# A norm's sum over the partitions: two dense products with ones, and the root on all partitions

## The chip, the cores and the metric

The kernel runs on one core of a Trainium2 chip. The metric is the time of one execution on the device in microseconds; the time of a kernel is the median of its runs. Five engines work side by side, each in the order of its own queue: TensorE (PE; its weight loads are shown as PEld), VectorE (DVE), ScalarE (ACT), GpSimd (POOL) and SyncE (SP, which here issues DMAs).

## The reference

The reference is an encoder of two layers on 512 positions of 1024 features. Each layer is a SwiGLU half-step, a mixer with three branches (a gated DeltaNet, pooling, dilated attention) and a second SwiGLU half-step. What matters here is the norm ahead of each of the three parts:

```python
def _rmsnorm(x, gain):
    xf = x.astype(jnp.float32)
    y = xf * lax.rsqrt(jnp.mean(xf * xf, axis=-1, keepdims=True) + RMS_EPS)
    return (y * gain.astype(jnp.float32)).astype(x.dtype)

for l in range(DEPTH):                      # DEPTH = 2
    x = x + 0.5 * _swiglu(_rmsnorm(x, ffn1_norm[l]), ...)
    h = _rmsnorm(x, mix_norm[l])
    ...
    x = x + 0.5 * _swiglu(_rmsnorm(x, ffn2_norm[l]), ...)
return _rmsnorm(x, final_norm)
```

## The kernel before

The activations lie with features on the partitions and positions along the columns: eight tiles `xs` of 128 x 512. A gemm (L238 to L253) makes one 128 x 512 output tile. Its operands are split into a high and a low part of type fp32r (`split`, L186: ScalarE rounds to the high part at L187, VectorE subtracts at L188). For each of the k blocks it issues three products, high by high (L246), high by low (L248) and low by high (L250); with the eight blocks of `xs` these are 24 products. The accumulator is one of three PSUM banks (pool `psA`). The weights come by DMA in blocks of 1024 columns and are split into pairs of 512 columns, of which four can stand ready (`weights`, L190, with the tags `wh` and `wl`).

The norm is not applied to the operand. `prep` (L257) multiplies a tile by the gain, splits it, and adds its squares to `ss` (128 x 512) by `square` (L264). The gemms work on the unnormed tiles, and each output column is multiplied by the factor R of its position when the accumulator is read out: L308 and L312 in the FFN, L407 and L375 in the mixer, L1085 for the gates. R is a 128 x 512 tile with the same row on all partitions.

`norm` (L285) computes R from `ss`. It calls `rms` (L289). For each of four blocks of 128 positions, that function multiplies a block of `ss` by a column of ones (L294), which puts the sum of each position on a partition of its own, in one column. The four columns go through mean and epsilon (L296) and through `rsqrt_cols` (L272: root on ScalarE, reciprocal and one Newton step on VectorE), all 128 x 4. Four transposes (L300) of the columns, each spread over 128, bring the factors back along the columns on all partitions, and L287 copies them into R. The last norm of the kernel is done by `down_last` (L332), which calls `rms` itself.

A planner of the framework sets the order on each engine from the order of the program, with an offset for parts marked as urgent (`high_priority`); `norm` and the read-outs of the mixer carry the largest offset, `AHEAD_E`, and the weights a smaller one, `AHEAD`. Within one queue an instruction that waits holds up all behind it. Tiles with the tag `t` (`T5`, `tt`) share four buffers, small PSUM tiles (`bank`) five.

In the mixer, `deltanet` (L386) begins with a short gemm for beta and decay (L404, L405), read out with R at L407. Then comes a chain of small steps on PE, DVE and ACT (L410 to L458), and then the twelve convolutions (`conv`, L370), each on a gemm's output, read out with R at L375 into a tile `t`.

Of the kernel before, what the change touches and what calls it, by code (L numbers as in the profile page):

```python
# [10 lines left out]
F32 = mybir.dt.float32  # L11
F32R = mybir.dt.float32r
AF = mybir.ActivationFunctionType
ALU = mybir.AluOpType
AX = mybir.AxisListType

P = 128
T = 512
D = 1024
# [4 lines left out]
RMS_EPS = 1e-6  # L24
# [77 lines left out]
def trunk(ctx: ExitStack, tc: tile.TileContext, A, out):  # L102
    nc = tc.nc
    V, S, G, PE = nc.vector, nc.scalar, nc.gpsimd, nc.tensor
    PSUM = bass.MemoryType.PSUM

    pc = ctx.enter_context(tc.tile_pool(name="pc", bufs=1))
# [11 lines left out]
    def nm(s):  # L119
        uid[0] += 1  # L120
        return f"{s}_{uid[0]}"

    def T5(dt=F32):
        return pt_.tile([P, TW], dt, tag="t", name=nm("t"))

    def tt():
        return T5()[:, 0:T]
# [10 lines left out]
    def bank():  # L138
        return psM.tile([P, T], F32, tag="m", name=nm("m"))

    def small(w, tag, bufs=2):
        return pc.tile([P, w], F32, tag=tag, bufs=bufs, name=nm(tag))

    def f32(ap):
        return ap.bitcast(F32)
# [4 lines left out]

    cst = pc.tile([P, NCONST], F32, name="cst")
    gain = pc.tile([P, (3 * DEPTH + 1) * NB], F32, name="gain")
    pc.tile([P, 8], F32, name="pad")
    eps = pc.tile([P, 2], F32, name="eps")
    V.memset(eps[:, 0:1], RMS_EPS)
    V.memset(eps[:, 1:2], 4.0 * L2_EPS)
    ones = pc.tile([P, 2], F32, name="ones")
    V.memset(ones, 1.0)

    def C(n):  # L160
        o, w = CONST[n]
        return cst[:, o:o + w]
# [5 lines left out]
    ss = pc.tile([P, T], F32, name="ss")  # L168
    R = pc.tile([P, T], F32, name="R")
# [16 lines left out]
    def split(raw, h, l):  # L186
        S.activation(h, raw, AF.Copy)  # L187
        V.tensor_tensor(out=l, in0=raw, in1=f32(h), op=ALU.subtract)  # L188
# [83 lines left out]
    def rsqrt_cols(v, n):  # L272
        y = small(n, "rs1")
        u = small(n, "rs2")
        S.activation(u, v, AF.Sqrt)  # L275
        V.reciprocal(y, u)  # L276
        V.scalar_tensor_tensor(out=u, in0=y, scalar=-0.5, in1=y, op0=ALU.mult, op1=ALU.mult)
        V.tensor_tensor(out=u, in0=u, in1=v, op=ALU.mult)
        V.scalar_tensor_tensor(out=y, in0=u, scalar=1.5, in1=y, op0=ALU.add, op1=ALU.mult)
        return y  # L280
# [2 lines left out]
        S.activation(small(1, "jk"), col, AF.Sqrt, scale=0.0, bias=ones[:, 0:1])  # L283

    def norm():  # L285
        with tc.high_priority(offset=AHEAD_E):
            V.tensor_copy(R, rms([ss], 0, 4))  # L287

    def rms(parts, b0, b1):  # L289
        n = b1 - b0  # L290
        p = bank()
        for b in range(b0, b1):
            for i, t in enumerate(parts):
                PE.matmul(p[:, b:b + 1], t[:, b * P:(b + 1) * P], ones[:, 0:1], start=(i == 0), stop=(i == len(parts) - 1))  # L294
        v = small(4, "nv")[:, 0:n]
        V.tensor_scalar(out=v, in0=p[:, b0:b1], scalar1=1.0 / D, scalar2=RMS_EPS, op0=ALU.mult, op1=ALU.add)  # L296
        y = rsqrt_cols(v, n)
        q = bank()
        for b in range(n):
            PE.transpose(q[:, b * P:(b + 1) * P], y[:, b:b + 1].to_broadcast([P, P]), ident)  # L300
        return q[:, 0:n * P]
# [889 lines left out]
    for l in range(DEPTH):  # L1191
        norm()
        ffn(A["f1g"][l], A["f1u"][l], A["f1d"][l], xs, 3 * l + 1, True)
        norm()
        xs = mixer(l, 3 * l + 2)
        norm()
        last = l == DEPTH - 1
        ffn(A["f2g"][l], A["f2u"][l], A["f2d"][l], xs, None if last else 3 * l + 3, False)
# [59 lines left out]
```

## Time and profile before

| | |
|---|---|
| median of 3 runs | 2571.84 us (2570.33 to 2571.87) |
| profiled execution | 2572.03 us |
| its span | 2570.2 us |
| instructions | 33959 |
| PE, PEld | 2548.9 us (99%), 2087.2 us (81%) |
| DVE, ACT, POOL | 1469.6 us (57%), 1002.9 us (39%), 164.0 us (6%) |

The span is the time between the first and the last instruction that the profile shows. Busy time is the time in which an engine has at least one instruction under way. Matmuls overlap, so that their durations add up to more than the time they take; what a matmul costs is the distance from one start to the next. In a timeline, the first number is the start in us from the start of the span, the second the duration.

### The profile page before, as it was taken

The numbers are of one execution on the slowest core, as the hardware profiler recorded it, in microseconds if no ns is written. First come the engines' busy times: TensorE is split into PE (matmuls) and PEld (weight loads), VectorE is DVE, ScalarE is ACT, GpSimd is POOL, SyncE is SP. The second block draws the span as 40 slices with busy tenths as digits, with TensorE's granted clock in tenths as the row PEclk, the third lists the DMA queues.
The fourth block names the chain that finished last, engine by engine and source line by source line (L and its number), as shares of the span: only waits on it lengthen the run. The fifth ranks groups of instructions, "written<-read, shape, count | busy, mean of one in ns | idle before, by whom it ended". The sixth has DMA issues, their size and how long they took to land. (4 is left out here: it accounts for less than half of the span.)

```text
span 2570.2 us, 33959 instructions
## 1 busy us (share of the span) xinstructions
PE 2548.9 (99%) x13018; PEld 2087.2 (81%) x13018; DVE 1469.6 (57%) x2702; ACT 1002.9 (39%) x1946; POOL 164.0 (6%) x117
## 2 busy tenths in 40 slices
PE   9999999999999999999999999999999999999998
PEld 7888887888878788888888888878888778888887
DVE  6444349956767654443444444499566576544433
ACT  5333234464443333333233332354644334333322
POOL 1000000001221200000000000000022112000010
PEclk9999999999999999999999999999999999999999
DMA  4222333232323522223322223323323244222232
GB/s 157 97 99 97 113 104 107 89 119 88 109 90 111 171 95 99 98 92 96 101 97 93 98 97 117 110 97 100 107 94 103 83 136 155 91 99 98 96 96 80
DMA packets 96051, 268.32 MB, mean 104 GB/s; under 512 B 14384, under 2 KB 19984, under 8 KB 95888
## 3 DMA queue, kind: packets, MB, share of 16 engines
q1 hardware_dynamic: 74928, 229.41, 27.1%
q10 hardware_dynamic: 20960, 36.75, 4.5%
q8 instruction: 102, 1.67, 0.3%
q14 instruction: 61, 0.50, 0.1%
HBM read 245.02 MB, written 14.79 MB: 101 GB/s over the span
## 5 line engine op out<-in xcount | busy, mean ns | idle before, releaser
L187 ACT ACTIVATE wh<-raw 128x512 fp32r<-128x512 f32 (+1 forms) x870 | 539.1, 620 | 1171.7 <-PE acc L248 1097.0
L250 PE MATMUL acc<-xh,wl 128*128 128x512 f32 x2400 | 941.1, 392 | 1.5 <-DVE wl L188 1.5
L246 PE MATMUL acc<-xh,wh 128*128 128x512 f32 x2400 | 940.7, 392 | 1.4 <-ACT wh L187 1.1
L248 PE MATMUL acc<-xl,wh 128*128 128x512 f32 x2400 | 939.9, 392 | 0.5 <-DVE xl L1175 0.3
L188 DVE TENSOR_TENSOR wl<-raw,wh 128x512 fp32r<-128x512 f32 (+1 forms) x870 | 604.2, 694 | 540.2 <-ACT wh L187 534.9
L250 PEld LDWEIGHTS acc<-xh,wl 128*128 128x128 f32 x2400 | 451.0, 188 | 99.0 <-issue 3.5
L246 PEld LDWEIGHTS acc<-xh,wh 128*128 128x128 f32 x2400 | 451.1, 188 | 98.9 <-issue 2.9
L248 PEld LDWEIGHTS acc<-xl,wh 128*128 128x128 f32 x2400 | 450.8, 188 | 97.1 <-issue 2.6
L246 PE MATMUL acc<-r,wh 128*128 128x512 f32 x970 | 379.2, 391 | 6.9 <-DVE f L1137 6.9
L250 PE MATMUL acc<-r,wl 128*128 128x512 f32 x970 | 379.1, 391 | 0.0
L248 PE MATMUL acc<-r,wh 128*128 128x512 f32 x970 | 379.0, 391 | 0.0
L246 PEld LDWEIGHTS acc<-r,wh 128*128 128x128 f32 x970 | 182.9, 189 | 46.1 <-issue 7.7
L248 PEld LDWEIGHTS acc<-r,wh 128*128 128x128 f32 x970 | 182.7, 188 | 38.3 <-issue 0.3
L250 PEld LDWEIGHTS acc<-r,wl 128*128 128x128 f32 x970 | 182.9, 189 | 38.1
L312 DVE TENSOR_TENSOR t<-acc,R 128x512 f32<-128x512 f32 x88 | 60.9, 692 | 132.1 <-PE acc L250 132.1
L308 DVE TENSOR_TENSOR f<-acc,R 128x512 f32<-128x512 f32 x88 | 60.9, 692 | 128.1 <-PE acc L250 127.9
L187 ACT ACTIVATE r<-t 128x512 fp32r<-128x512 f32 x96 | 60.4, 631 | 128.6 <-DVE t L313 127.5
L188 DVE TENSOR_TENSOR r<-t,r 128x512 fp32r<-128x512 f32 x96 | 69.8, 729 | 60.8 <-ACT r L187 60.7
L591 POOL MEMSET r<- 128x1024 f32 x2 | 1.9, 953 | 1107.9 <-PE acc L250 1107.9
L379 DVE SCALAR_TENSOR_TENSOR f<-t,cw,f 128x512 f32<-128x512 f32 x96 | 69.4, 744 | 0.0
L309 ACT ACTIVATE f<-f 128x512 f32<-128x512 f32 x88 | 55.7, 632 | 23.0 <-DVE f L308 23.0
L313 DVE TENSOR_TENSOR t<-t,f 128x512 f32<-128x512 f32 x88 | 60.5, 688 | 1.3 <-ACT f L309 1.3
(281 smaller groups left out, 1692.8 us busy)
## 6 DMA issues: line engine op xcount, KB each, us to landing
raw<-in_win_dram SPq DMA_DIRECT2D x76, 512.0 KB, 3.3
raw<-in_wgt_dram SPq DMA_DIRECT2D x48, 512.0 KB, 3.3
raw<-in_f2g_dram SPq DMA_DIRECT2D x44, 512.0 KB, 3.2
raw<-in_f2u_dram SPq DMA_DIRECT2D x44, 512.0 KB, 3.2
raw<-in_f1g_dram SPq DMA_DIRECT2D x43, 512.0 KB, 3.2
raw<-in_f1u_dram SPq DMA_DIRECT2D x43, 512.0 KB, 3.2
raw<-in_f1d_dram SPq DMA_DIRECT2D x32, 512.0 KB, 3.4
raw<-in_f2d_dram SPq DMA_DIRECT2D x32, 512.0 KB, 3.5
```

The costliest lines, as they stand in the source:

```text
L187: S.activation(h, raw, AF.Copy)
L188: V.tensor_tensor(out=l, in0=raw, in1=f32(h), op=ALU.subtract)
L246: PE.matmul(acc, a, h, start=(k == 0), stop=False)
L248: PE.matmul(acc, a, l, start=False, stop=False)
L250: last = PE.matmul(acc, b, h, start=False, stop=(k == nk - 1))
L308: V.tensor_tensor(out=g1, in0=g, in1=R, op=ALU.mult)
L309: S.activation(g1, g1, AF.Silu)
L312: V.tensor_tensor(out=u1, in0=u, in1=R, op=ALU.mult)
L313: V.tensor_tensor(out=u1, in0=u1, in1=g1, op=ALU.mult)
L379: V.scalar_tensor_tensor(out=a, in0=cp[:, j:j + T], scalar=w[:, j:j + 1], in1=a, op0=ALU.mult, op1=ALU.add)
L591: G.memset(X_, 0.0)
```

## The change

Only `norm` is changed. The tile `pad`, which nothing used, gives way to `onesr`, ones of type fp32r. `ss` is split into a high and a low part (128 x 512 each); both are multiplied by a 128 x 128 matrix of ones, made by repeating one column of `onesr`, and accumulated in one PSUM bank. This puts the sum of each position on all partitions at once. Mean and epsilon, the root, the reciprocal and the Newton step then run on the full 128 x 512 tile and end in R. The transposes and the copy L287 are gone from `norm`; `rms` stays for the last tile.

```diff
-    pc.tile([P, 8], F32, name="pad")
+    onesr = pc.tile([P, 2], F32R, name="onesr")
...
     V.memset(ones, 1.0)
+    V.tensor_copy(onesr, ones)
...
     def norm():
+
         with tc.high_priority(offset=AHEAD_E):
-            V.tensor_copy(R, rms([ss], 0, 4))
+            h, lo = T5(F32R)[:, 0:T], T5(F32R)[:, 0:T]
+            split(ss, h, lo)
+            p = bank()
+            on = onesr[:, 0:1].to_broadcast([P, P])
+            PE.matmul(p, on, h, start=True, stop=False)
+            PE.matmul(p, on, lo, start=False, stop=True)
+            V.tensor_scalar(out=ss, in0=p, scalar1=1.0 / D, scalar2=RMS_EPS, op0=ALU.mult, op1=ALU.add)
+            u = tt()
+            S.activation(u, ss, AF.Sqrt)
+            V.reciprocal(R, u)
+            V.scalar_tensor_tensor(out=u, in0=R, scalar=-0.5, in1=R, op0=ALU.mult, op1=ALU.mult)
+            V.tensor_tensor(out=u, in0=u, in1=ss, op=ALU.mult)
+            V.scalar_tensor_tensor(out=R, in0=u, scalar=1.5, in1=R, op0=ALU.add, op1=ALU.mult)
```

## Rows read from the trace of the kernel before

**Rows 1.** Page, part 1 (busy) and part 2 (TensorE's granted clock).

```profile
PE 2548.9 (99%) x13018; PEld 2087.2 (81%) x13018; DVE 1469.6 (57%) x2702; ACT 1002.9 (39%) x1946; POOL 164.0 (6%) x117
...
PEclk9999999999999999999999999999999999999999
```

**Rows 2.** Waits of TensorE: line, releaser, total us, times, longest.

```profile
PE acc L246 <- ACT wh L187: 1.1, 2, 0.5
```

**Rows 3.** Groups by line and shape, TensorE, the two lines of the old norm.

```profile
L294 PE MATMUL m<-ones,ss 128*128 128x1 f32 x56 | 7.5, 247 | 0.0
...
L300 PE MATMUL m<-ident,rs 128*128 128x128 f32 x28 | 4.6, 282 | 1.4 <-DVE rs L279 1.4
```

**Rows 4.** Timeline of TensorE, norm ahead of the second FFN: start, duration.

```profile
923.42 0.39 PE L246 MATMUL acc<-xh,wh 128*128 128x512 f32 x1
...
926.05 1.02 PE L294 MATMUL m<-ones,ss 128*128 128x1 f32 x8
...
933.44 0.39 PE L248 MATMUL acc<-xl,wh 128*128 128x512 f32 x1
...
944.55 0.39 PE L250 MATMUL acc<-xh,wl 128*128 128x512 f32 x1
```

**Rows 5.** Groups by line and shape, VectorE: busy us, mean ns of one.

```profile
L260 DVE SCALAR_TENSOR_TENSOR xl<-mg,gain,xh 128x512 fp32r<-128x512 f32 x40 | 29.9, 748 | 0.2
L270 DVE TENSOR_TENSOR ss<-ss,t 128x512 f32<-128x512 f32 x41 | 28.2, 689 | 0.6
...
L287 DVE COPY R<-m 128x512 f32<-128x512 f32 x6 | 4.1, 687 | 0.9 <-PE m L300 0.9
...
L276 DVE RECIPROCAL rs<-rs 128x4 f32<-128x4 f32 x6 | 1.1, 176 | 0.8 <-ACT rs L275 0.5
L276 DVE RECIPROCAL rs<-rs 128x16 f32<-128x16 f32 x4 | 1.0, 250 | 2.7 <-ACT rs L275 2.7
...
L430 DVE RECIPROCAL sp<-sp 128x32 f32<-128x32 f32 x2 | 0.7, 353 | 2.3 <-ACT sp L427 2.3
```

**Rows 6.** Groups by line and shape, ScalarE.

```profile
L187 ACT ACTIVATE wh<-raw 128x512 fp32r<-128x512 f32 x823 | 519.6, 631 | 1081.5 <-PE acc L248 1011.0 <-DVE wl L188 23.3 <-issue 10.3
```

**Rows 7.** Timeline of VectorE, the same norm as rows 4.

```profile
925.22 0.69 DVE L270 TENSOR_TENSOR ss<-ss,t 128x512 f32<-128x512 f32 x1
...
932.05 0.69 DVE L308 TENSOR_TENSOR f<-acc,R 128x512 f32<-128x512 f32 x1
```

**Rows 8.** Timeline of VectorE, norm ahead of the mixer, and after it.

```profile
373.37 0.69 DVE L270 TENSOR_TENSOR ss<-ss,t 128x512 f32<-128x512 f32 x1
...
377.71 0.68 DVE L287 COPY R<-m 128x512 f32<-128x512 f32 x1
...
389.05 0.28 DVE L458 COPY t<-m 32x128 f32<-32x128 f32 x1 [0.39 <-PE m L456]
389.27 0.67 DVE L375 TENSOR_TENSOR t<-acc,R 128x512 f32<-128x512 f32 x1
...
427.31 0.69 DVE L375 TENSOR_TENSOR t<-acc,R 128x512 f32<-128x512 f32 x1
```

**Rows 9.** Window of VectorE between the last two rows: length, busy us.

```profile
389.27:427.31 38.04, 34.70 (x65) 1.00 0.35 112
```

**Rows 10.** Timeline of TensorE around the end of that window.

```profile
427.23 0.39 PE L250 MATMUL acc<-xh,wl 128*128 128x512 f32 x1
428.15 0.47 PE L246 MATMUL acc<-xh,wh 128*128 128x512 f32 x1 [0.53 <-ACT wh L187]
```

**Rows 11.** Timeline of VectorE, the kernel's first norm.

```profile
18.99 0.68 DVE L1185 TENSOR_TENSOR ss<-ss,t 128x512 f32<-128x512 f32 x1
...
25.44 0.69 DVE L308 TENSOR_TENSOR f<-acc,R 128x512 f32<-128x512 f32 x1
```

**Rows 12.** Timeline of TensorE, the same stretch.

```profile
19.50 0.39 PE L248 MATMUL acc<-xl,wh 128*128 128x512 f32 x1
...
28.85 0.39 PE L246 MATMUL acc<-xh,wh 128*128 128x512 f32 x1
```

## The prediction, made before the changed kernel had run

> **What bounds the kernel now.** [...] Then TensorE's waits: no releaser holds it up for more than a few microseconds in all, and the row shown is one of the few [rows 2]. Then the timeline, to price one matmul: from 933.44 to 944.55 lie 49 starts, so one 128x512 product costs 0.2267 us, although the view gives each 0.39 us, because they overlap [rows 4]. So time is gained by taking work off TensorE's queue, and lost where that queue has to wait for something. The other engines matter only through such a wait.
>
> A norm is called six times: ahead of the first FFN, of the mixer and of the second FFN, in two layers. The 56 passes of L294 and the 28 of L300 hold a few of the last tile's as well, which keeps the old code; 48 and 24 belong to the six norms [rows 3].
>
> **What leaves TensorE.** Their own durations overlap, so I price them by the delay of the gemm around them. Ahead of the second FFN, between 923.42 and 933.44, 37 gemm products start; at 0.2267 us they fill 8.39 of 10.02 us, so the old norm takes 1.63 us of TensorE there [rows 4]. At the kernel's first norm 35 starts fill 7.93 of 9.35 us: 1.42 us [rows 12]. I use 1.63 for the three norms ahead of an FFN that follows other gemms (two second FFNs, layer 1's first), and 1.42 for the first norm and the two ahead of a mixer.
>
> **What comes to TensorE.** Two products with a 512-column moving operand of the same type as the gemm's: 2 x 0.2267 = 0.45 us. Each waits for a fresh result (ScalarE's high part, VectorE's low part). The nearest wait is the old one: the product before L294 was the 11th from 923.42, so L294 was due at 925.91 and started at 926.05, 0.14 us late [rows 4]. Bounds: nothing, if the planner places them after their data, and below nothing no way is seen; above, 0.35 us each, two and a half times that row. I take 0.14 each: 0.73 us a norm. Saved: 0.90 us at three norms, 0.69 at the other three, 4.8 us in all, if nothing waits for the norm's result R.
>
> **When R is ready.** The old chain ran on 4 columns; the new one runs on 512, nine steps behind one another. High part 0.63 (ScalarE, as rows 6), low part 0.69 (as L270), the last product 0.39, mean and epsilon out of PSUM 0.69 (as L287), root 0.63, reciprocal, then 0.75, 0.69 and 0.75 (as L260 and L270) [rows 4 to 6]. The reciprocal at 512 columns is not in the trace. At 4, 16 and 32 columns it takes 176, 250 and 353 ns, 6.2 to 6.4 ns a column, against 689 ns for a whole 512-column add [rows 5]. Carried on from 32 columns at about 6.3 ns: 353 + 480 x 6.3 = 3.4 us. [...] I take 3.4, since three rows of the same instruction lie on one line. The sum is 8.6 us, and six hand-overs at an estimated 0.05 us make 8.9. One weight split of 0.69 us (VectorE's L188, which works in order) may get in front, so 8.9 to 9.6.
>
> [...]
>
> **Who waits for R, place by place.** A gemm has 24 products (5.44 us) and three PSUM accumulators rotate, so TensorE stops only when a fourth gemm finds none read out.
> Ahead of the FFNs: the sum of squares ends at 925.22 + 0.69 = 925.91, R would come at 934.8 to 935.5 and the first eviction L308 end by 936.2, against 932.74 before [rows 7]. The fourth gemm starts 72 products after 923.42, so at 923.42 + 16.32 + 0.73 = 940.5 [rows 4]. Some 4 us to spare: no loss, 0.90 saved, three times: -2.7 us.
> The first norm: the sum ends at 19.67 [rows 11]. R at 28.6 to 29.3, and one more split would make it 30.0; L308 takes 0.69, and TensorE goes on 0.14 later. The fourth gemm started at 28.85, its 73rd product [rows 12], and would now be due 0.69 earlier. It would start between 29.4 and 30.8 instead; I take one split, so 30.1: +1.2 us.
> Ahead of the mixer: the sum ends at 374.06 and R was written at 378.39 [rows 8]. Now 383.0 to 383.7, some 5 us later. The chain of small steps from R to L458 sets the time of the first convolution's eviction L375, right behind L458 in VectorE's order, 10.9 us after R [rows 8]; it moves by the same 5 us. From there VectorE is nearly full: busy 34.70 of 38.04 us until the eviction at 427.31 [rows 9], which frees an accumulator at 428.00. TensorE's next product starts at 428.15, where 427.46 was due [rows 8, 10]. The row names ScalarE's split as the releaser; the accumulator was free 0.15 us before the start, and I take that as what it waited for. So here VectorE already sets TensorE's pace, and the 0.69 us saved ahead is lost in this wait. Of the 5 us, the idle 3.3 us can be used up, and two weight splits (one each 2.72 us of TensorE, 2 x 0.69 = 1.4) fit into VectorE's longer wait before L375: slip 0.3 us at best, 5 at worst. I take 1.0, near the lower end, because the gaps are mostly waits for splits that TensorE's own progress releases, and those will have come by then. Twice: +2.0 us.
>
> **Other engines.** VectorE gets 7.0 us of new work a norm and loses the copy L287 (0.69) and five tiny steps (about 0.16 each), net 5.5; ScalarE gets two wide steps for one tiny one. Behind VectorE's three waits (for ScalarE, TensorE, ScalarE) and the long reciprocal stand the weight splits; four buffered pairs at 2.72 us each cover 8 us of TensorE. Without that cover a split stuck behind the reciprocal would cost up to 3.4 us. Behind ScalarE's wait for the mean stand the high parts of weights, held 1.8 us at most, under the same cover. DMAs are neither added nor moved, though SP's weight loads wait for their buffers, and so follow late splits under that cover too.
>
> **Sum.** -2.7 + 1.2 + 2.0 = +0.5 us on the profiled execution's 2572.03 (span 2570.2 and 1.8 around it): 2572.5. The median shown is 0.2 below that execution, so 2572.3. With each term's bounds (three FFN norms -1.4 to -3.5, the first norm +0.5 to +1.9, the two mixers together +0.6 to +5) the likeliest case alone spans 2569.5 to 2577.
>
> **Rivals.**
> R is not late. If the wide reciprocal costs about 0.69 us, the chain is 2.7 us shorter. The first norm's R comes at about 26, early enough, and the mixers' slip of about 2.3 is taken up by the idle time, so that the eviction at 427.31 keeps its place (its 0.69 us are not gained either). Then 2.7 + 0.7 = 3.4 us stay saved: 2568.4. With no wait at the new products and the eviction earlier as well it would be 6 x 1.53 - 2.7 = 6.5: 2565.3. Against it speaks the line of three reciprocal rows.
> VectorE's delay is not absorbed (the slower side). If the gaps after 389.27 stay, because they are waits in order behind ScalarE, the eviction at 427.31 comes the full 5 us late in each layer: +10 + 1.2 - 2.7 = +8.5, so 2580.3. It decides from a slip of about 3.3 us a layer, where the total passes 5.1. For it: VectorE has 91% of that window busy and works in order; against it: the splits that wait there are paced by TensorE.
> [...]
>
> **How the numbers follow.** Likeliest case 0.55, R not late 0.15, delay not absorbed 0.17, eight element times 0.13. About 5.1 us (0.2%) is what a measurement of this kernel can tell from no change, so faster means under 2566.7 and slower over 2577.0. Faster: a quarter of the second case and a sliver of the first, 0.05. Slower: nearly all of the third, some of the fourth, a few hundredths of the first, 0.20. The rest, 0.75, is no change. The range goes from 2566.5 to 2580: about half of the third case and a bit of the second stay outside.
>
> **What would show it.** [...] The norm's TensorE share at the second FFN, counted as above: 0.73 us instead of 1.63. The fourth gemm's first product at about 30. The product that stood at 428.15, 1 us late against its own layer's start, rather than 5. R to L308 without a gap on TensorE ahead of the FFNs. I am wrong in the mechanism if TensorE waits nowhere for R, or if it waits directly behind the norm in its own queue for longer than 0.35 us, at the new products or at L410.

## The result: 2585.5 us, slower by 0.54%, and the profile after

| | before | after |
|---|---|---|
| median | 2571.87 us (2570.33 to 2572.35, 6 runs) | 2585.49 us (2584.09 to 2588.17, 6 runs) |
| span of the profiled execution | 2570.2 us | 2584.0 us |
| ratio after to before | | 1.0054, 95% interval 1.0043 to 1.0066 |

The prediction was 2572.3 us, with a range of 2566.5 to 2580: wrong, by 13.2 us. All line numbers below are those of the changed kernel, unless another is named. There `norm` has its two products at L293 and L294, mean and epsilon at L295, the root at L297, the reciprocal at L298 and the Newton step at L299 to L301. The splits are L188 and L189, a gemm's products L247, L249 and L251, the read-outs L322 and L326 (FFN, before L308 and L312), L421 and L389 (mixer, before L407 and L375).

The page after, parts 1 and 2, shows next to nothing of the loss. It answers to [rows 1]:

```profile
PE 2548.7 (99%) x12958; PEld 2084.2 (81%) x12958; DVE 1496.7 (58%) x2703; ACT 1007.8 (39%) x1951; POOL 163.9 (6%) x117
...
PEclk9999999999999999999999999999999999999999
```

TensorE is busy 99% of both spans, and a slice of 65 us hides a clock that is low for 3 us. The waits of TensorE (line, releaser, total us, times, longest) do show it:

```profile
PE acc L247 <- DVE t L389: 11.8, 4, 5.1
PE acc L247 <- DVE f L1151: 7.0, 2, 3.5
PE acc L247 <- DVE f L322: 3.4, 1, 3.4
```

The second row stands in the kernel before as well, as its largest wait:

```profile
PE acc L246 <- DVE f L1137: 6.9, 2, 3.5
```

The first and the third are new, 15.2 us in all: a gemm that finds no accumulator free, because an earlier one is not read out with R yet.

To place the loss I compared the start of the same gemm product, by its number in the queue, in both traces. The delay goes from about 0 to +4.6 us at the first norm (0.45 of it arises in the kernel's first 11 us, before the norm), to +11.0 over layer 0's mixer, falls by 1.0 at layer 0's second FFN and by 1.0 at layer 1's first, rises by 7.6 at layer 1's convolutions, falls by 1.6 further on in the same mixer, and by 1.0 at the last FFN. So: first norm +4.6, mixers +6.3 and +5.9, the other three norms -2.9, sum +13.9 (spans: +13.8).

**The steps of the norm.** Groups by line and shape after (busy us, mean ns of one), VectorE:

```profile
L298 DVE RECIPROCAL R<-t 128x512 f32<-128x512 f32 x6 | 20.1, 3352 | 5.1 <-ACT t L297 4.8
...
L295 DVE TENSOR_SCALAR ss<-m 128x512 f32<-128x512 f32 x6 | 4.1, 691 | 1.8 <-PE m L294 1.8
```

L299, L300 and L301 take 678, 683 and 689 ns. The reciprocal takes 3.35 us, where 3.4 was worked out from three narrow ones [rows 5].

**The first norm.** Timeline of VectorE after (start, duration; in brackets the idle time before and its releaser). It answers to [rows 11]:

```profile
19.45 0.68 DVE L1199 TENSOR_TENSOR ss<-ss,t 128x512 f32<-128x512 f32 x1
20.06 1.28 DVE L189 TENSOR_TENSOR wl<-raw,wh 128x512 fp32r<-128x512 f32 x2
21.40 0.69 DVE L189 TENSOR_TENSOR t<-ss,t 128x512 fp32r<-128x512 f32 x1
...
23.33 0.69 DVE L295 TENSOR_SCALAR ss<-m 128x512 f32<-128x512 f32 x1 [0.64 <-PE m L294]
...
24.72 3.35 DVE L298 RECIPROCAL R<-t 128x512 f32<-128x512 f32 x1
27.99 0.63 DVE L189 TENSOR_TENSOR wl<-raw,wh 128x512 fp32r<-128x512 f32 x1
28.54 0.68 DVE L299 SCALAR_TENSOR_TENSOR t<-R 128x512 f32<-128x512 f32 x1
29.13 0.68 DVE L189 TENSOR_TENSOR wl<-raw,wh 128x512 fp32r<-128x512 f32 x1
...
30.45 0.69 DVE L301 SCALAR_TENSOR_TENSOR R<-t,R 128x512 f32<-128x512 f32 x1
...
31.18 0.69 DVE L322 TENSOR_TENSOR f<-acc,R 128x512 f32<-128x512 f32 x1
```

From the end of the sum (19.45 + 0.68 = 20.13) to R (31.14) pass 11.0 us. No step is longer than it was taken, but six weight splits stand among them in VectorE's order. Those at 27.99 and 29.13 hold the chain up by 0.5 us each. Its start is held up by 0.6 us: the norm's own high part starts on ScalarE only at 20.75, behind a weight's high part at 20.21, and VectorE spends that time on the two splits at 20.06. (The other two, left out of the rows, fit into the chain's waits.) Also, L294 started on TensorE at 22.90, 0.8 us after the low part was there (21.40 + 0.69). TensorE has meanwhile filled its three accumulators. Its timeline, which answers to [rows 12]:

```profile
28.16 0.39 PE L251 MATMUL acc<-xh,wl 128*128 128x512 f32 x1
31.92 0.80 PE L247 MATMUL acc<-xh,wh 128*128 128x512 f32 x1 [3.38 <-DVE f L322]
...
35.07 0.39 PE L249 MATMUL acc<-xl,wh 128*128 128x512 f32 x1
```

Two losses stand in these rows. One is the wait. The other is the distance of starts behind it: 0.60 us for the first, then 0.43 until 35.07 (these rows are left out), 0.23 from there on. Windows of TensorE (window, length, busy, instructions, granted clock, DMA):

```profile
20.00:28.00 8.00, 8.00 (x37) 1.00 0.78 262
...
31.90:35.00 3.10, 3.08 (x7) 0.50 0.22 87
35.00:36.00 1.00, 1.00 (x6) 0.98 0.00 0
```

After the idle stretch the granted clock is 0.50 for about 3.1 us, against 1.00 from 20 to 28. The 7 starts from 31.92 on take 3.15 us until the next one at 35.07, where 7 x 0.2267 = 1.59 would do: 1.6 us lost beside the wait.

**The mixer.** Timeline of VectorE after, norm ahead of layer 0's mixer, beside [rows 8]:

```profile
378.01 0.68 DVE L271 TENSOR_TENSOR ss<-ss,t 128x512 f32<-128x512 f32 x1
...
387.96 0.69 DVE L301 SCALAR_TENSOR_TENSOR R<-t,R 128x512 f32<-128x512 f32 x1
...
399.73 0.28 DVE L472 COPY t<-m 32x128 f32<-32x128 f32 x1
399.96 0.67 DVE L389 TENSOR_TENSOR t<-acc,R 128x512 f32<-128x512 f32 x1
...
433.15 0.69 DVE L189 TENSOR_TENSOR wl<-raw,wh 128x512 fp32r<-128x512 f32 x1 [1.31 <-ACT wh L188]
...
436.84 0.68 DVE L389 TENSOR_TENSOR t<-acc,R 128x512 f32<-128x512 f32 x1
```

From the end of the sum to R: 10.0 us, against 4.3 before. To the first convolution's read-out L389: 21.3 us, against 15.2, so that slips by 6.1. The window from there to the read-out that frees the next accumulator answers to [rows 9]:

```profile
399.96:436.84 36.88, 33.82 (x64) 1.00 0.39 115
```

It is only 1.2 us shorter than before, and VectorE's idle time in it is 3.06 us, against 3.34. The idle time was hardly used up: it is waits in VectorE's order, such as the 1.31 us at 433.15 for ScalarE. Thus 4.9 us of the slip arrive at TensorE, in the row that answers to [rows 10]:

```profile
400.78 0.47 PE L247 MATMUL acc<-xh,wh 128*128 128x512 f32 x1 [0.85 <-DVE t L389]
...
432.23 0.39 PE L251 MATMUL acc<-xh,wl 128*128 128x512 f32 x1
437.67 0.63 PE L247 MATMUL acc<-xh,wh 128*128 128x512 f32 x1 [5.05 <-DVE t L389]
438.10 0.63 PE L249 MATMUL acc<-xl,wh 128*128 128x512 f32 x1
...
441.39 0.40 PE L247 MATMUL acc<-xh,wh 128*128 128x512 f32 x1
```

Here too starts stand 0.43 us apart after the wait, until 441 (granted clock 0.53 from 437.60 to 441.00): the 9 starts to 441.39 take 3.72 us in place of 2.04, and 1.7 are lost. Layer 0's mixer is then -0.8 (norm) + 0.85 + 4.5 (5.05 less the old 0.53) + 1.7 = +6.3, as the products' delay says.

Layer 1 shows the same two waits, 0.85 us at 1678.46 and 5.05 us at 1715.33, but a longer stretch at the low clock. A row of TensorE's timeline and two windows, the second right behind its second wait of 3.5 us for L1151:

```profile
1715.33 0.77 PE L247 MATMUL acc<-xh,wh 128*128 128x512 f32 x1 [5.05 <-DVE t L389]
```

```profile
1715.30:1721.20 5.90, 5.87 (x14) 0.50 0.00 0
...
2132.50:2136.50 4.00, 3.99 (x18) 1.00 0.47 143
```

The 14 starts from 1715.33 to the next one at 1721.36 take 6.03 us in place of 3.17, so 2.9 are lost, and the sum is +7.4 (the products' delay: +7.6). The 1.6 us that the delay falls further on stand behind another wait. The kernel before runs at the low clock behind both of its waits for L1137 (0.55 from 842.80 to 846.60, 0.56 from 2115.90 to 2119.80); the changed kernel does so behind its first wait for L1151 (granted clock 0.56 from 853.80 to 857.60), but behind the second, of the same length, the clock stands at 1.00. Why it differs isn't shown.

**The norms ahead of the other FFNs** pay, as predicted. Timeline of TensorE after, second FFN of layer 0, beside [rows 4]:

```profile
934.38 0.39 PE L247 MATMUL acc<-xh,wh 128*128 128x512 f32 x1
...
937.60 0.50 PE L293 MATMUL m<-t,onesr 128*128 128x512 f32 x1
...
938.39 0.43 PE L294 MATMUL m<-t,onesr 128*128 128x512 f32 x1
...
945.95 0.39 PE L247 MATMUL acc<-xh,wh 128*128 128x512 f32 x1
```

From the first to the last of these rows 48 gemm products start, 10.88 of 11.57 us: the norm takes 0.69 us of TensorE.

### The profile page after: what moved, and what is told of

It reads as the page before. It is cut to its first block, busy times and chain, and to the rows that moved or that the text cites. A ratio compares the mean times of both kernels' runs of the same rounds, so it can differ in the third digit from the quotient of the medians.

```text
span 2584.0 us, 33850 instructions
## 1 busy us (share of the span) xinstructions
PE 2548.7 (99%) x12958; PEld 2084.2 (81%) x12958; DVE 1496.7 (58%) x2703; ACT 1007.8 (39%) x1951; POOL 163.9 (6%) x117
## 5 line engine op out<-in xcount | busy, mean ns | idle before, releaser
L188 ACT ACTIVATE wh<-raw 128x512 fp32r<-128x512 f32 (+1 forms) x870 | 539.1, 620 | 1159.7 <-PE acc L249 1082.9
L247 PE MATMUL acc<-xh,wh 128*128 128x512 f32 x2400 | 944.2, 394 | 15.5 <-DVE t L389 11.8
L251 PE MATMUL acc<-xh,wl 128*128 128x512 f32 x2400 | 942.4, 393 | 1.5 <-DVE wl L189 1.5
L249 PE MATMUL acc<-xl,wh 128*128 128x512 f32 x2400 | 941.4, 392 | 0.4 <-DVE xl L1189 0.3
L189 DVE TENSOR_TENSOR wl<-raw,wh 128x512 fp32r<-128x512 f32 (+1 forms) x870 | 602.5, 693 | 531.9 <-ACT wh L188 530.4
L247 PEld LDWEIGHTS acc<-xh,wh 128*128 128x128 f32 x2400 | 452.6, 189 | 114.5 <-ACT t L395 10.9
L251 PEld LDWEIGHTS acc<-xh,wl 128*128 128x128 f32 x2400 | 452.4, 189 | 98.9 <-issue 3.5
L249 PEld LDWEIGHTS acc<-xl,wh 128*128 128x128 f32 x2400 | 452.3, 189 | 98.2 <-DVE xl L1189 2.9
L247 PE MATMUL acc<-r,wh 128*128 128x512 f32 x970 | 378.8, 390 | 7.0 <-DVE f L1151 7.0
L251 PE MATMUL acc<-r,wl 128*128 128x512 f32 x970 | 378.4, 390 | 0.0
L249 PE MATMUL acc<-r,wh 128*128 128x512 f32 x970 | 378.2, 390 | 0.0
L247 PEld LDWEIGHTS acc<-r,wh 128*128 128x128 f32 x970 | 182.5, 188 | 46.0 <-issue 7.7
L249 PEld LDWEIGHTS acc<-r,wh 128*128 128x128 f32 x970 | 182.5, 188 | 37.8 <-issue 0.3
L251 PEld LDWEIGHTS acc<-r,wl 128*128 128x128 f32 x970 | 182.4, 188 | 37.9
L326 DVE TENSOR_TENSOR t<-acc,R 128x512 f32<-128x512 f32 x88 | 60.8, 691 | 128.2 <-PE acc L251 128.2
L322 DVE TENSOR_TENSOR f<-acc,R 128x512 f32<-128x512 f32 x88 | 60.8, 691 | 123.3 <-PE acc L251 123.3
L188 ACT ACTIVATE r<-t 128x512 fp32r<-128x512 f32 x96 | 60.4, 632 | 124.2 <-DVE t L327 123.1
L189 DVE TENSOR_TENSOR r<-t,r 128x512 fp32r<-128x512 f32 x96 | 69.8, 729 | 59.5 <-ACT r L188 59.4
L323 ACT ACTIVATE f<-f 128x512 f32<-128x512 f32 x88 | 55.6, 632 | 24.3 <-DVE f L322 24.2
```

Source lines behind the costliest of these rows:

```text
L247: PE.matmul(acc, a, h, start=(k == 0), stop=False)
L249: PE.matmul(acc, a, l, start=False, stop=False)
L251: last = PE.matmul(acc, b, h, start=False, stop=(k == nk - 1))
L322: V.tensor_tensor(out=g1, in0=g, in1=R, op=ALU.mult)
L323: S.activation(g1, g1, AF.Silu)
L326: V.tensor_tensor(out=u1, in0=u, in1=R, op=ALU.mult)
```

## The experiments

Four theories stood against one another. A: R comes late, TensorE waits for an accumulator at the first norm and in each mixer, and runs at the low clock after it; at the other three norms there is a gain. B: the loss is spread over all norms (the products, or another order by the planner). C: it is VectorE's added load, not R's delay. D: `h`, `lo` and `u` take buffers from the other tiles `t`.

**The new norm at some places only.** The other places keep the old one. These are three runs, which the comments of the edit call e1 to e3; the expectations stand in this order.

```diff
-    def norm():
+    def norm(new=True):
+        if not new:
+            with tc.high_priority(offset=AHEAD_E):
+                V.tensor_copy(R, rms([ss], 0, 4))
+            return
...
-        norm()
+        norm(l > 0)      # e1; e2: l == 0; e3: False
...
-        norm()
+        norm(False)      # e1; e2: False; e3: True
...
-        norm()
+        norm(True)       # e1; e2: False; e3: False
```

> New norm only ahead of the two second FFNs and of layer 1's first FFN; the old one at the kernel's first norm and ahead of both mixers. Theory A (R comes late, TensorE waits for a free accumulator at the first norm and in each mixer, and at the other three places it only gains): three times 1.0 us gained, 2568.9 against 2571.9 before. Theory B (the loss lies in the dense products themselves or in the planner's other order, so it is spread over all six norms, 13.6/6 = 2.3 us each): 2578.7.

Measured: 2569.98 us against 2572.21, ratio 0.9988 (0.9979 to 0.9996). The three norms alone are faster than the kernel before, by 2.2 us where 3.0 were expected. In the profiled execution each of them gives 1.0 by the products' delay; 0.8 is lost in the first 15 us, before any new norm, and 0.9 by a longer stretch at the low clock behind the wait for L1154 (L1151 here).

> New norm only at the kernel's first norm. Theory A: TensorE waits some 3.4 us for the first accumulator and then runs about 3 us at the lower clock, less 0.5 saved: +4.6 us, 2576.5. Theory B (a sixth of the loss): +2.3, 2574.2.

Measured: 2576.18, ratio 1.0015 (1.0005 to 1.0024): +4.0 us.

> New norm only ahead of the two mixers. Theory A: TensorE waits about 5 us in each layer for the accumulator behind the convolutions and then runs at the lower clock for some 3 us, about 6.4 us a layer: +12.8, 2584.7. Theory B (two sixths of the loss): +4.5, 2576.4.

Measured: 2584.94, ratio 1.0052 (1.0037 to 1.0068): +12.7 us, 6.4 a mixer. Waits of TensorE, first of the run with the first norm alone, then of the one with the mixers alone (L325 and L392 are L322 and L389 here):

```profile
PE acc L247 <- DVE f L325: 3.4, 1, 3.4
```

```profile
PE acc L247 <- DVE t L392: 11.8, 4, 5.1
```

The three parts add up: -2.2 + 4.0 + 12.7 = +14.5, where the whole gave +13.6. Each new wait appears with its own norm and in its full length. B is refuted.

**The reciprocal away.**

```diff
-            V.reciprocal(R, u)
-            V.scalar_tensor_tensor(out=u, in0=R, scalar=-0.5, in1=R, op0=ALU.mult, op1=ALU.mult)
+            V.tensor_scalar(out=R, in0=u, scalar1=0.0, scalar2=0.05, op0=ALU.mult, op1=ALU.add)
+            V.scalar_tensor_tensor(out=u, in0=R, scalar=-1e-9, in1=R, op0=ALU.mult, op1=ALU.mult)
```

> New norm everywhere, with a 128x512 tensor_scalar in place of the wide reciprocal and the Newton factor made tiny; R is then a constant 0.075 and the output is not the reference's. The chain is about 2.9 us shorter. Theory A: the first norm's wait shrinks from 3.4 to about 0.5 us and its low clock goes, the mixers' waits shrink from 5 to about 2.2 us, with no low clock: about +0.2 + 2 x 1.7 - 3.0 = +0.6, 2572.5. Theory B: as the changed kernel, 2585. Theory C (VectorE's added work, 5.5 us a norm, is what counts, wherever it stands): half of the work stays, about half of the loss, 2578.

Measured: 2573.32, ratio 1.0004 (0.9995 to 1.0013). The stand-in takes 428 ns, so the chain is 2.9 us shorter. At the first norm TensorE starts its fourth gemm only 0.2 us late, and in each mixer it waits for R once, shorter. Its timeline in layer 0:

```profile
429.65 0.47 PE L247 MATMUL acc<-xh,wh 128*128 128x512 f32 x1 [2.93 <-DVE t L389]
429.96 0.40 PE L249 MATMUL acc<-xl,wh 128*128 128x512 f32 x1
430.19 0.40 PE L251 MATMUL acc<-xh,wl 128*128 128x512 f32 x1
```

After 2.93 us of waiting the starts stay 0.23 us apart: no low clock. By the products' delay the mixers cost 1.5 and 1.8 us here. Against 6.3 and 7.6 (behind R's wait) that is 4.8 and 5.8 less, and 2.9 of chain with 1.7 and 2.9 of clock are 4.6 and 5.8. This sizes both of A's terms, though C could claim the 2.9 us of VectorE as well; the next run parts them.

**R late without VectorE.** The kernel before, with R copied onto itself by ScalarE at the first norm and ahead of both mixers.

```diff
-    def norm():
+    def norm(late=0):
         with tc.high_priority(offset=AHEAD_E):
             V.tensor_copy(R, rms([ss], 0, 4))
+            for _ in range(late):
+                S.activation(R, R, AF.Copy)
...
-        norm()
+        norm(8 if l == 0 else 0)
...
-        norm()
+        norm(8)
```

> The old norm, with R copied onto itself eight times by ScalarE (8 x 0.63 = 5.0 us) at the kernel's first norm and ahead of both mixers: R comes about as late as in the changed kernel, VectorE gets no work and TensorE saves nothing. Theory A (lateness of R): the first norm loses about 2.5 us of waiting and 1.6 of low clock, each mixer about 5 and 1.6: +4 + 2 x 6.5 = +17, 2589. Theory C (VectorE's added work): within 2 us of before, 2572 to 2574.

Measured: 2592.77, ratio 1.0081 (1.0066 to 1.0096). Waits of TensorE (L377 and L310 are the read-outs of the mixer and of the FFN):

```profile
PE acc L246 <- DVE t L377: 10.1, 2, 5.1
...
PE acc L246 <- DVE f L310: 4.8, 1, 4.8
```

With the old, small norm and no added work on VectorE the same two waits appear, and the mixer's is as long as in the changed kernel. C is not needed for the loss. The time is 3.8 us above what was expected, since the first norm alone lost 7.8 us: its wait was 4.8 us, as R came at 33.05 (two weights' high parts and a load of ScalarE's function table, 1.28 us, stood between the copies in its queue), and the clock was low behind it for nearly 6 us, which cost 2.8. A window of TensorE behind that wait:

```profile
33.80:39.60 5.80, 5.77 (x14) 0.50 0.00 0
```

**Tiles of their own.**

```diff
-            h, lo = T5(F32R)[:, 0:T], T5(F32R)[:, 0:T]
+            hl = ring(F32R)
+            h, lo = hl[:, 0:T], hl[:, T:2 * T]
...
-            u = tt()
+            u = tf()
```

> The changed kernel, with the norm's three tiles taken from other pools than the four buffers with the tag t, from which the convolutions' tiles come. Theory A: no change against the changed kernel, 2585. Theory D (the norm holds three of the four t buffers, and so the first eviction in the mixer comes late): the first eviction L389 moves back by several us, the mixers' loss of 12.8 shrinks by more than half, 2578 or less.

Measured: 2587.76, ratio 1.0061 (1.0044 to 1.0078), and the changed kernel's waits are all there (L390 and L323 are the mixer's and the FFN's read-out):

```profile
PE acc L247 <- DVE t L390: 11.8, 4, 5.1
...
PE acc L247 <- DVE f L323: 3.4, 1, 3.4
```

The first read-out L390 of layer 0's mixer starts 12.0 us after R's last step (387.68 and 399.68), as in the changed kernel (387.96 and 399.96). D is refuted. This run is 2.3 us slower than the changed kernel; in its profiled execution the clock is low in layer 0's mixer for longer, 0.50 from 400.4 to 403.8 and from 438.0 to 444.7.

**A fourth accumulator**, in the changed kernel and in the one before.

```diff
-    psA = ctx.enter_context(tc.tile_pool(name="psA", bufs=3, space=PSUM))
-    psM = ctx.enter_context(tc.tile_pool(name="psM", bufs=5, space=PSUM))
+    psA = ctx.enter_context(tc.tile_pool(name="psA", bufs=4, space=PSUM))
+    psM = ctx.enter_context(tc.tile_pool(name="psM", bufs=4, space=PSUM))
```

> The changed kernel with four gemm accumulators instead of three, and four small PSUM tiles instead of five. Theory A: a fourth accumulator gives TensorE 5.4 us more before it must wait, more than each of the three waits, so these and the low clock behind them go and the saving of some 0.9 us a norm is left: 2567. Theory B: 2585.

> The kernel before with the same division of PSUM, for the run above. Theory A: only the two short waits of 0.69 us in the mixers go, 2570.5. If the fifth small PSUM tile is needed elsewhere, slower than before by some microseconds, here as there.

Measured: the changed kernel 2573.31, ratio 1.0006 (0.9997 to 1.0015); the kernel before 2570.53, ratio 0.9992 (0.9983 to 1.0001). With four accumulators the changed kernel is 2.8 us slower than the kernel before with as many, where with three it is 13.6. Giving TensorE the accumulator that it waited for takes 10.8 us of the loss away, which bears A out. But I had expected 2567, all six norms paying, and that is a miss of 6 us. And that the kernel before meets its 2570.5 is in part luck. The two short waits in the mixers are gone, as expected (0.6 and 0.7 us); but the waits for L1137 fall too, from 6.9 to 2.0 us, and with them the low clock behind them, 8 us in all by the products' delay, and nearly as much is lost again at other places. Waits of TensorE in the mixers of the changed kernel with four accumulators:

```profile
PE acc L247 <- DVE t L389: 2.3, 2, 1.2
PE m L634 <- DVE r L616: 2.2, 2, 1.1
...
PE m L673 <- ACT r L678: 1.4, 2, 0.7
PE m L659 <- ACT t L637: 1.3, 4, 0.4
PE m L521 <- DVE r L397: 1.3, 2, 0.8
...
PE m L545 <- DVE f L397: 0.6, 2, 0.3
```

These are 9.1 us. The kernel before with four accumulators has 1.5 us of such waits (1.3 at its counterpart of L673, 0.2 at that of L545). The difference is 7.6 us; less 0.8 saved at each norm it leaves 6.0 for the two mixers. By the products' delay between these two runs they cost 4.4 and 0.8 us, and the second is 1.6 too small, since the kernel before with four accumulators runs at the low clock there for a while (0.50 from 1813.7 to 1817.1) and the changed one does not: together 6.8. So it seems that the accumulator was only the first place where late read-outs reached TensorE: behind it wait the deltanet's own products (L521 to L673), whose operands come from the same read-outs. No run takes these waits away.

**What pays, together.** The three norms of the first run and the fourth accumulator.

> The new norm at the three places where its factor is not late (both second FFNs, layer 1's first FFN), and four gemm accumulators in place of three (the small PSUM tiles get four banks for five). If the two are independent, the three norms give 2572.21 - 2569.98 = 2.2 us as in the run with them alone, and the division of the PSUM 2.0 us as in the run of the kernel before with it (ratio 0.9992): 2571.9 - 4.2 = 2567.7. With 1.0 us a norm by the delay counted product by product it is 2566.9. Rival: with a fourth accumulator the norm's products only move into time that TensorE had to spare further on, so that one of the two gains is had but once: 2569.5 to 2570.

Measured: 2565.95 us against 2571.93, ratio 0.9978 (0.9969 to 0.9987), the fastest kernel of this study. It lies 1.8 us below the sum, so the two at least don't take from each other. Why it is more is not shown, but the clock is likely to have a part in it. Single runs of the three norms alone spread from 2565.93 us, with a granted clock of 0.999 over the run, to 2570.82 with 0.996. And in the profiled executions the stretch at the low clock from 1813.7 on, 1.6 us, is in the kernel before with four accumulators and not in this one.

## Why the prediction was wrong

- **What leaves and comes to TensorE: right.** 0.69 us a norm, where 0.73 was worked out; the three FFN norms gave -2.9 by the products' delay, where -2.7 was predicted, and R was awaited at none of them.
- **The reciprocal: right.** 3.35 us for 3.4. That is (3352 - 353) / 480 = 6.25 ns a column beyond the 32-column row of [rows 5], so the line of the three narrow rows held out to 512. The price of a plain add, 0.69, is refuted. The chances also name a fourth case, eight element times (0.13): no run shows that term, and what they showed in its place is the 3.35 us.
- **When R is ready: too early.** 11.0 us at the first norm and 10.0 at the mixer, where 8.9 to 9.6 stood. The steps were right; what stands between them was not. The 0.05 us of a hand-over were an estimate that no row gave; at the first norm the root starts 0.04 us after L295 ends (24.02 and 24.06) and the reciprocal 0.03 after the root ends (24.69 and 24.72). One split was allowed for, and at the first norm weight splits held the chain up at three places and its second product came 0.8 us late. A chain of nine steps gives other work nine chances to get in front.
- **The first norm: mis-sized.** +1.2 was predicted, from R at 29.3 and TensorE going on at 30.1 in the likeliest case. R came at 31.14 and TensorE went on at 31.92. Its wait was 3.4 us, and with the low clock (1.6), what was saved by the norm (-0.9) and what was lost before it (0.45) that makes +4.5, near the +4.6 of the products.
- **The mixers: the step that failed.** The prediction saw the chain L410 to L458 and the read-out L375 behind it, and VectorE busy 34.70 of 38.04 us [rows 9]. Then it took a slip of 1.0 us, near the lower end of 0.3 to 5, because the idle 3.3 us could be used up and two splits could move ahead. The first read-out slipped 6.1 us and 4.9 of them arrived. VectorE's idle time behind the first read-out stayed (3.06 of 3.34 us); no more than 1.2 us of the slip was taken up. The prediction's third case (VectorE's delay is not absorbed) said just that. Its price, 5 us a layer, was short by the low clock.
- **Not in the prediction at all: the clock.** Each of the three new waits is followed by a stretch at a granted clock of about half (0.50, 0.53 and 0.50 in windows of 3.1, 3.4 and 5.9 us), which costs 1.6, 1.7 and 2.9 us. The kernel before has two such stretches, of about 1.6 us each, behind its two waits of 3.5 us for L1137, and the changed kernel only one, so that the clock adds 4.5 us net. The prediction showed one of the small waits [rows 2] and left out the largest, whose 6.9 us are more than the "few microseconds in all" that it allows any releaser; the low clock could have been read behind it. A window of TensorE in the kernel before, layer 1:

```profile
2115.90:2119.80 3.90, 3.87 (x10) 0.56 0.49 137
```

Ten starts fill 3.90 us, where 2.27 would do.

Of the +13.8 us of span +0.5 was predicted. By the products' delay the other terms were short by about 9.0 us (the first norm by 1.9, the mixers by 7.3, the other norms better by 0.2) and the clock makes up 4.5. The chances leaned on the lower bound of an unknown cost (0.55 for it, 0.17 for the upper), although the row next to it, VectorE at 91% and working in order, spoke for the upper one.

## What to carry to other kernels

TensorE's 99% hides whether a result is awaited: before a chain that ends in a factor is made longer, count for each place how long the accumulators let TensorE run without the read-out, and reckon with the whole delay as lost where the engine that reads out works in order and is nearly full (here 4.9 of 6.1 us). Idle time of an engine inside a dependent chain is not slack until it is known what each gap waits for. A change that is good at three places and bad at three is worth having at the three; and waits on TensorE such as those of 3.4 to 5 us here are to be priced with the clock that may fall behind them (0, 1.6 or 2.9 us here).

## What the runs showed of the hardware

The wide reciprocal on VectorE costs 3352 ns for 128 x 512, some 4.9 times an add of the same size (689 ns, L270 before); the trace before showed it at 176, 250 and 353 ns for 4, 16 and 32 columns.

After waits of 3.38 and 5.05 us TensorE's granted clock stood at about 0.50 for about 3 us, and behind another wait of 5.05 us for about 6; a 128 x 512 product then took 0.43 us from start to start where it takes 0.2267. These falls cost 1.6, 1.7 and 2.9 us. The length of the wait alone does not decide: behind waits of 3.48 us for the same line the clock fell once (at 853.80, to 0.56 over 3.8 us) and once not (at 2132.51, 1.00 over 4.0 us) in the same execution. After the two waits of 2.93 us in the run without the reciprocal (until 429.65 and 1702.63) the starts stayed 0.23 us apart. The page's digits of the clock, means over 65 us, stood at 9 throughout.
